# A decoder layer on one core: single-column norm factors move from VectorE to ScalarE, and the FFN weight sums become a step of their own

## The chip, the core and the metric

The kernel runs on one core of a Trainium2 chip. The core's engines work side by side, each on its own instruction queue, and wait for one another by semaphores: PE (TensorE, matmuls and transposes), DVE (VectorE), ACT (ScalarE), POOL (GpSimd) and SP (SyncE, which only issues DMAs here). The metric is the device time of one execution in microseconds. All tensors are float32, one batch of 1024 tokens, width 1024.

## The reference, cut to what matters

The layer has three residual blocks. Before each, every row is normalised: divided by the root of its mean square plus EPS, times a gain.

```python
def rmsnorm(x, g):
    xf = x.astype(jnp.float32)
    y = xf * lax.rsqrt(jnp.mean(xf * xf, axis=-1, keepdims=True) + EPS)
    return (y * g.astype(jnp.float32)).astype(x.dtype)

def reference(x, mem, ...):
    ...
    h = h + token_mixer(rmsnorm(h, g_mix[l]), ...)                       # top-k sparse + differential attention
    h = h + cross_attention(rmsnorm(h, g_xattn[l]), rmsnorm(mem, g_mem[l]), ...)  # 4 heads, 256 memory tokens, w_xo
    h = h + conv_glu(rmsnorm(h, g_ffn[l]), w_ffn_in[l], conv_w[l], conv_b[l], w_ffn_out[l])

def conv_glu(hn, w_ffn_in, conv_w, conv_b, w_ffn_out):
    a, gate = jnp.split(hn @ w_ffn_in, 2, axis=-1)        # 1024 x 1024 times 1024 x 5632
    ...                                                   # causal convolution of width 3 over the tokens
    return (jax.nn.gelu(conv) * gate) @ w_ffn_out
```

## The kernel before

Rows of tokens are handled in eight tiles of 128 (t = 0 to 7). Products in float32 are made of three matmuls each (`mm3`, L287 to L289): every operand is split into a high part, which a cast rounds, and a low part, which is the remainder; high by high, high by low and low by high are added in PSUM. So for each weight and each activation somebody makes a cast (ACT, or POOL) and a subtraction (DVE, or POOL).

**Norm factors.** `rstd` makes 1/sqrt(mean square + EPS) without a square root: a first guess by integer arithmetic on the bits and two polynomial steps. On DVE this is nine instructions (L107, L108, L110 to L116) on a tile of 128 rows by n columns. `norm_rows` calls it with one column, behind an ACT instruction that squares a row tile and sums it (L1113). It is called sixteen times: in `x_norm` for the eight tiles of the cross attention's input, and in `f_norm` for the eight tiles of the FFN's input. In `f_norm` the scaling at L1293 (h times factor times gain, two halves of 512 columns) follows. Other callers of `rstd` have two or more columns.

**The way into the FFN.** `xo_unit(1, t)` is the second half of the cross attention's output projection for tile t: 24 matmuls, and L1278 adds the result to h. In its middle stands `f_tr(t - 2)`, which transposes the scaled tile t − 2 on PE (L1359, two groups of four 128 x 128 transposes, one PSUM bank each of the two banks called trp). For tiles 0 to 3 the banks are split into high and low (cast L1310, subtraction L1313, into B11 and B21). For tiles 4 to 7 one bank is split into B22, and both go into sums and differences for a Strassen-like scheme: L1324 adds high and low back (`xb_sum`), L1372 and L1374 subtract on DVE and read the banks, L1376 and L1378 subtract on POOL. Behind the last tile `xb_finish` splits the sums T1 to T3 (cast L1338, subtraction L1339).

The FFN's input has 22 tiles of 128 columns of a and of the gate (f = 0 to 21). One tile takes seven products of 12 matmuls (`product`), with the weights' sums and differences as one factor and B11, B21, B22, T1 to T4 as the other. Its results pass through three kinds of PSUM buffers (acc, trp, big).

**Weights.** The class `Weights` holds a list of jobs in the order of use. `pump(1)` works off the next job if there is room among the twelve split pages; `get` forces jobs until the pages asked for are there. For one FFN tile there are four jobs: A splits both halves of the first load and, behind that, forms the sums and differences of both loads in place (L204 to L206); B, C and D split the rest (L212 is one more difference). L181 is the cast, L184 the subtraction on DVE. Each load is 512 KB into one of three raw buffers, issued by SP when a buffer comes free.

**What sets the order.** The order of an engine's instructions is fixed when the kernel is built: a scheduler with a model of the chip's times orders DVE, ACT, POOL and SP over the whole program. Only in one block the order of PE is that of the code (`manual_schedule`): there the eight `xo_unit(1, t)` with their transposes, then the first FFN tile, with the last two transposes between its products:

```python
for t in range(NT):
    xo_unit(1, t, (lambda: f_tr(t - 2)) if t >= 2 else None)
    f_norm(t)
first = ffn_in(0)
next(first)
f_tr(6)
next(first)
f_tr(7)
next(first)
```

Each `next` is a product: B11, B21, and B22, which needs tile 7.

Of the kernel before, what the change touches and what calls it, by code (L numbers as in the profile page):

```python
# [12 lines left out]
I32 = mybir.dt.int32  # L13
AF = mybir.ActivationFunctionType
OP = mybir.AluOpType
# [3 lines left out]
P = 128  # L19
T = 1024  # L20
D = 1024
# [5 lines left out]
EPS = 1e-6  # L27
# [17 lines left out]
def hybrid_layer(ctx, tc, I, out):  # L45
    nc = tc.nc
    pe, act, dve, pool, sp = nc.tensor, nc.scalar, nc.vector, nc.gpsimd, nc.sync
# [13 lines left out]
    def nm(s):  # L61
        cnt[0] += 1
        return f"{s}_{cnt[0]}"
# [16 lines left out]
    def small(name, shape=(P, 8), bufs=8):  # L80
        return wpool.tile(list(shape), F32, name=nm(name), tag=name, bufs=bufs)
# [20 lines left out]
    def rstd(eng, r, ss, n, scale):  # L102


        w = small("rst", (P, 3, 8), 4) if n <= 8 else rt("hl", [P, 3, 64], F32, "rstw")
        m, y, t = w[:, 0, :n], w[:, 1, :n], w[:, 2, :n]
        eng.tensor_scalar(m, ss, scale, EPS, op0=OP.mult, op1=OP.add)  # L107
        eng.tensor_scalar(y.bitcast(I32), m.bitcast(I32), -0.5, 1597463007.0, op0=OP.mult, op1=OP.add)  # L108
        if eng is dve:
            eng.scalar_tensor_tensor(t, y, -3.0 / 16, y, op0=OP.mult, op1=OP.mult)  # L110
            eng.tensor_tensor(t, t, m, op=OP.mult)
            eng.scalar_tensor_tensor(y, t, 9.0 / 16, y, op0=OP.add, op1=OP.mult)
            eng.scalar_tensor_tensor(t, y, 64.0 / 9, y, op0=OP.mult, op1=OP.mult)
            eng.tensor_tensor(t, t, m, op=OP.mult)
            eng.scalar_tensor_tensor(t, t, -10.0 / 3, t, op0=OP.add, op1=OP.mult)
            eng.scalar_tensor_tensor(r, t, 5.0, y, op0=OP.add, op1=OP.mult)  # L116
        else:
            eng.tensor_tensor(t, y, y, op=OP.mult)
            eng.tensor_tensor(t, t, m, op=OP.mult)
            eng.tensor_scalar(t, t, -3.0 / 16, 9.0 / 16, op0=OP.mult, op1=OP.add)  # L120
            eng.tensor_tensor(y, t, y, op=OP.mult)
            eng.tensor_tensor(t, y, y, op=OP.mult)
            eng.tensor_tensor(t, t, m, op=OP.mult)
            eng.tensor_scalar(m, t, 64.0 / 9, -10.0 / 3, op0=OP.mult, op1=OP.add)
            eng.tensor_tensor(t, t, m, op=OP.mult)
            eng.tensor_scalar(t, t, 64.0 / 9, 5.0, op0=OP.mult, op1=OP.add)
            eng.tensor_tensor(r, t, y, op=OP.mult)


    NRAW, NWP = 2, 12  # L130

# [12 lines left out]
    class Weights:  # L144
# [41 lines left out]
        def split(self):  # L186
            i = self.nsplit
            key, src, n, engines, kind, _ = self.jobs[i]
            while src is not None and i not in self.raws:
                self.load()  # L190
            raw = self.raws.pop(i, None)
            fi = self.fi

            def fpart(x):
                self.parts(self.page(key), x, 512, engines[0])
            if kind == "A":
                fi["a"] = raw
                fpart(raw[:, 0, :])
                fpart(raw[:, 1, :])
                if i + 1 not in self.raws:  # L200
                    self.load()
                a, g = raw, self.raws[i + 1]
                fi["s"] = s1 = page_s()
                dve.tensor_tensor(s1, g[:, 0, :], g[:, 1, :], op=OP.add)  # L204
                dve.tensor_tensor(g[:, 0, :], a[:, 0, :], g[:, 0, :], op=OP.subtract)
                dve.tensor_tensor(a[:, 0, :], s1, a[:, 0, :], op=OP.subtract)  # L206
            elif kind == "B":
                fi["g"] = raw
                a = fi["a"]
                fpart(a[:, 0, :])  # L210
                fpart(fi["s"])
                dve.tensor_tensor(a[:, 1, :], a[:, 1, :], a[:, 0, :], op=OP.subtract)  # L212
            elif kind == "C":
                fpart(fi["g"][:, 0, :])
                fpart(fi["a"][:, 1, :])
            elif kind == "D":
                fpart(fi["g"][:, 1, :])
            elif kind == "memT":
                for j in range(2):
                    pg = self.page(key)  # L220
                    for b in range(2):
                        v = slice(256 * b, 256 * b + 256)
                        gk = gmem[:, n + 2 * j + b:n + 2 * j + b + 1]
                        act.activation(pg[:, 0, v], raw[:, j, v], AF.Copy, scale=gk)
                        dve.scalar_tensor_tensor(pg[:, 1, v], raw[:, j, v], gk, pg[:, 0, v].bitcast(F32),
                                                 op0=OP.mult, op1=OP.subtract)
            elif kind == "xq":
                for j in range(2):
                    pg, gk = self.page(key), gxa[:, engines + j:engines + j + 1]
                    pool.tensor_scalar(pg[:, 0, :], raw[:, j, :], gk, 1.0, op0=OP.mult, op1=OP.mult)  # L230
                    dve.scalar_tensor_tensor(pg[:, 1, :], raw[:, j, :], gk, pg[:, 0, :].bitcast(F32), op0=OP.mult, op1=OP.subtract)
            else:
                for j in range(2):
                    self.parts(self.page(key), raw[:, j, :n], n, engines[j])
            self.nsplit += 1
            if len(self.raws) < NRAW - 1 + len(raw3) // 2 or self.nload < self.nsplit:
                self.load()
# [17 lines left out]
    W = Weights()  # L255
# [23 lines left out]
    FIW = ("a", "d")  # L279
    for f in range(FT):  # L280
        src = [I["w_ffn_in"][f, :, w, :].rearrange("p (a b) -> p a b", a=2) for w in range(2)]
        W.add(("fi", f), src[0], 512, (FIW,), "A")
        W.add(("fi", f), src[1], 512, (FIW,), "B")
        W.add(("fi", f), None, 512, (FIW,), "C")
        W.add(("fi", f), None, 512, (FIW,), "D", 1)
# [17 lines left out]
    def rt(tag, shape, dt, name):  # L303
        return rot.tile(shape, dt, name=nm(name), tag=tag, bufs=ROT[tag])
# [35 lines left out]
    for k in range(KT):  # L340
        raw = early.tile([P, T], F32, name=nm("xraw"), tag="xr", bufs=5)
# [590 lines left out]
    for s in range(-4, NB):  # L932
        h, i = b_units[max(s, 0)]
        m = s % NT
# [137 lines left out]
    for s in range(-2, NA + 3):  # L1072
        i, h = a_units[min(max(s, 0), NA - 1)]
# [20 lines left out]
        u = s - 2  # L1094
# [16 lines left out]
    def norm_rows(src, jk, ssq, r):  # L1111

        act.activation(jk, src, AF.Square, accum_out=ssq)  # L1113
        rstd(dve, r, ssq, 1, 1.0 / D)

    hx, hx_h = {}, {}

    def x_norm(t, jk):
        ht = kq([P, D], F32, "hld")
        sp.dma_start(ht, h_d[t * P:(t + 1) * P, :])  # L1120
        st = small("st", (P, 12), 6)
        norm_rows(ht, jk, st[:, 0:1], st[:, 1:2])
        dve.tensor_scalar(ht, ht, st[:, 1:2], None, op0=OP.mult)
        hx_h[t] = ht
# [43 lines left out]
    def page_s():  # L1168
        return pgp.tile([P, 512], F32, name=nm("ws"), tag="ws", bufs=1)
# [113 lines left out]
    def f_norm(t):  # L1283
        rs = slice(t * P, (t + 1) * P)
        act.dma_start(h2_d[rs, :], h2[t])
        st = small("st", (P, 12), 6)
        ws = [w2([P, 512], F32, "hn") for _ in range(1 if t >= 4 else 2)]
        norm_rows(h2[t], ws[0].bitcast(BF), st[:, 0:1], st[:, 1:2])
        hn = []
        for g in range(2):  # L1290
            hg = h2[t][:, g * 512:(g + 1) * 512]
            w = hg if t >= 4 else ws[g]
            dve.scalar_tensor_tensor(w, hg, st[:, 1:2], gff[g], op0=OP.mult, op1=OP.mult)  # L1293
            hn.append(w)
        hst[t] = hn
# [420 lines left out]
```

## Time and profile before

| | us |
|---|---|
| median of three runs | 1697.2 (1692.95 to 1699.25) |
| profiled execution | 1697.69 |
| its span, first to last instruction | 1695.9 |
| PE busy in the span | 1570.8 (93%) |
| DVE busy | 1296.0 (76%) |
| ACT busy | 736.7 (43%) |
| POOL busy | 666.8 (39%) |

The granted TensorE clock over the span is 0.977 of full speed. The stages follow each other in time: projections and the first two attentions until about 690 us, cross attention until about 940, the second half of its output projection with f_norm until about 1004, the entry to the FFN, FFN input until about 1475, FFN output until the end. A row of a timeline gives the start, the busy time, the engine, the line in the kernel, the operation, output and input tiles and, in square brackets, how long the engine had been idle and what ended it. A row of waits gives the engine and its waiting line, what it waited for, the sum in us, how often, and the longest.

### The profile page before, as it was taken

Reading aid. Unit: us, or ns where it says so; the run is one execution under the profiler, and the core shown is the slowest. Engines: PE = TensorE matmul, PEld = TensorE weight load, DVE = VectorE, ACT = ScalarE, POOL = GpSimd, SP = SyncE. Lnnn points to the kernel's source line nnn. Section 1 sums busy time; section 2 is a strip of 40 time slices with the busy share of each in tenths; the row PEclk is TensorE's granted clock in tenths of the full one; section 3 lists DMA queues with packets and bytes.
Section 4 is the critical chain, followed back from the end, with each engine's and each line's share of the span. In section 5 each row is a group of like instructions: output and inputs, shape, how many; then the busy total and the mean of one; then the engine's idle time right before and its main releaser. Section 6 shows DMA issues by size and latency. Waiting matters only on the chain.

```text
span 1695.9 us, 22395 instructions
## 1 busy us (share of the span) xinstructions
PE 1570.8 (93%) x7660; PEld 1284.2 (76%) x7660; DVE 1296.0 (76%) x2524; ACT 736.7 (43%) x1469; POOL 666.8 (39%) x908
## 2 busy tenths in 40 slices
PE   8899988878889989999999978999999999899999
PEld 7788766667778778878777766887777777778887
DVE  5736998999999987467553588999988888665554
ACT  6545576566655326325442234333333333343432
POOL 2746666545440230140100032556666566541121
PEclk9999999899989999999999989999999999999999
DMA  8321225222230212261202121555544554698812
GB/s 284 94 82 58 71 93 163 73 62 78 90 100 26 70 68 69 71 220 63 75 25 88 62 87 65 179 174 191 174 164 166 179 180 167 251 366 320 315 50 75
DMA packets 112161, 220.05 MB, mean 130 GB/s; under 512 B 18480, under 2 KB 38448, under 8 KB 112048
## 3 DMA queue, kind: packets, MB, share of 16 engines
q1 hardware_dynamic: 91072, 148.37, 26.5%
q0 software_dynamic: 18384, 61.36, 10.3%
q10 hardware_dynamic: 2592, 8.91, 1.4%
q8 instruction: 60, 0.98, 0.2%
q14 instruction: 53, 0.43, 0.1%
HBM read 160.92 MB, written 57.67 MB: 129 GB/s over the span
## 4 chain that ended last, share of the span: by engine, by line
PE 47%; DVE 31%; DMA 8%; issue 6%; POOL 5%; ACT 3%; SPq 0%; ACTq 0%; DVEq 0%; POOLq 0%
PE acc L287 8%; PE acc L288 8%; PE acc L289 8%; DVE jk L544 6%; DVE wp L184 4%; PE big L288 3%; PE big L287 3%; PE big L289 3%; DMA fs<-u_d 2%; POOL fs L1529 2%; PE trp L287 2%; PE trp L288 2%; PE trp L289 2%; PE big L1255 2%; DMA raw<-in_w_ffn_in_dram 2%
## 5 line engine op out<-in xcount | busy, mean ns | idle before, releaser
L184 DVE TENSOR_TENSOR wp<-raw,wp 128x512 fp32r<-128x512 f32 (+1 forms) x200 | 192.9, 973 | 21.8 <-ACT wp L181 13.2
L181 ACT CAST wp<-raw 128x512 fp32r<-128x512 f32 (+1 forms) x188 | 110.1, 614 | 173.3 <-DVE raw L206 121.4
L1580 DVE TENSOR_TENSOR wp<-fo,wp 128x1024 fp32r<-128x1024 f32 x77 | 100.6, 1322 | 76.8 <-ACT wp L1579 75.2
L1529 POOL TENSOR_TENSOR fs<-fs,fs 128x512 f32<-128x512 f32 x88 | 126.8, 1441 | 77.6 <-DMA fs<-u_d 56.8
L1579 ACT CAST wp<-fo 128x1024 fp32r<-128x1024 f32 x77 | 79.8, 1049 | 108.9 <-PE big L289 47.0
L287 PE MATMUL acc<-wp,xh 128*128 128x512 f32 (+1 forms) x272 | 110.3, 407 | 9.4 <-ACT X L625 9.4
L183 POOL TENSOR_SCALAR wp<-raw 128x512 fp32r<-128x512 f32 (+1 forms) x64 | 46.7, 740 | 177.5 <-DVE rst L110 63.4
L289 PE MATMUL acc<-wp,xl 128*128 128x512 f32 (+1 forms) x272 | 109.8, 404 | 0.0
L288 PE MATMUL acc<-wp,xh 128*128 128x512 f32 (+1 forms) x272 | 109.5, 404 | 0.0
L661 ACT COPY pt<-trp 128x512 f32<-128x512 f32 (+3 forms) x144 | 65.6, 476 | 69.0 <-PE trp L670 68.5
L184 POOL TENSOR_TENSOR wp<-raw,wp 128x512 fp32r<-128x512 f32 x52 | 69.2, 1349 | 45.7 <-ACT wp L181 45.6
L1016 PEld LDWEIGHTS acc<-va_t,pt 128*128 128x128 f32 x576 | 74.0, 195 | 7.1 <-ACT pt L661 5.0
L1016 PE MATMUL acc<-va_t,pt 128*128 128x65 f32 x576 | 76.6, 273 | 2.6 <-ACT pt L661 2.0
L1626 POOL TENSOR_TENSOR hr<-hr,r 128x512 f32<-128x512 f32 x16 | 26.9, 1692 | 123.0 <-DMA fo<-ws_d 59.6
L1061 POOL DMA_DIRECT2D h_d<-xr x16 | 9.3, 579 | 165.6 <-DVE xr L1060 147.3
L999 ACT ACTIVATE ea<-ea,sta 128x128 f32<-128x128 f32 (+7 forms) x64 | 49.3, 777 | 49.8 <-DVE sta L998 46.4
L287 PEld LDWEIGHTS acc<-wp,xh 128*128 128x128 f32 x272 | 53.0, 195 | 23.0 <-ACT X L625 11.6
L544 DVE TENSOR_SCALAR_CACHE_REDUCE jk<-mb,cx 128x640 bf16<-128x640 uint16 (+1 forms) x64 | 68.6, 1072 | 0.7
L1482 POOL TENSOR_TENSOR fg<-fc,fg 128x1024 f32<-128x1024 f32 x21 | 50.9, 2425 | 36.3 <-ACT fc L1477 36.1
L544 DVE TENSOR_SCALAR_CACHE_REDUCE jk<-mb,cand 128x640 bf16<-128x640 bf16 (+3 forms) x60 | 64.4, 1073 | 0.4
L288 PE MATMUL acc<-wp,wp 128*128 128x512 f32 x152 | 61.2, 403 | 2.8 <-DVE wp L184 2.8
L1474 ACT ACTIVATE fc<-fa,cw 128x1024 f32<-128x1024 f32 x22 | 27.4, 1245 | 81.9 <-DVE fa L1433 72.2
(419 smaller groups left out, 5140.6 us busy)
## 6 DMA issues: line engine op xcount, KB each, us to landing
raw<-in_w_ffn_in_dram SPq DMA_DIRECT2D x44, 512.0 KB, 4.2
fs<-in_w_ffn_out_dram POOLq DMA_DIRECT2D x44, 256.0 KB, 3.8
ws_d<-fs POOLq DMA_DIRECT2D x44, 256.0 KB, 2.3
fs<-u_d POOLq DMA_DIRECT2D x44, 256.0 KB, 3.8
us_d<-fs POOLq DMA_DIRECT2D x44, 256.0 KB, 2.9
fo<-us_d SPq DMA_DIRECT2D x44, 256.0 KB, 5.3
fo<-ws_d SPq DMA_DIRECT2D x44, 256.0 KB, 5.4
u_d<-fg POOLq DMA_DIRECT2D x21, 512.0 KB, 4.4
```

Of the source, the lines that this page charges most:

```text
L181: act.copy(pg[:, 0, :n], src)
L184: (dve if el == "d" else pool).tensor_tensor(pg[:, 1, :n], src, pg[:, 0, :n].bitcast(F32), op=OP.subtract)
L287: pe.matmul(o, lhsT=lh, rhs=rh, start=start, stop=False)
L288: pe.matmul(o, lhsT=lh, rhs=rl, start=False, stop=False)
L289: pe.matmul(o, lhsT=ll, rhs=rh, start=False, stop=stop)
L544: dve.tensor_scalar(jk[:, :n], src, th[:, j:j + 1], None, op0=OP.is_ge, op1=OP.add, accum_out=cnt[:, j:j + 1])
L661: act.copy(dst, src)
L1016: pe.matmul(acc[:, hh * 65:hh * 65 + 65], lhsT=pt, rhs=va_t[:, kt, :], start=kt == 0, stop=kt == i)
L1482: pool.tensor_tensor(g, cv, g, op=OP.mult)
L1529: pool.tensor_tensor(o, p, q, op=op)
L1579: act.copy(hi, raw)
L1580: dve.tensor_tensor(lo, raw, hi.bitcast(F32), op=OP.subtract)
```

## The change

`norm_rows` calls a new function `rstd1`. Its first two steps stay on DVE; the rest, seven instructions on DVE before, are ten ACT instructions of one column (`AF.Copy` gives in times scale plus bias). Where a factor is itself a column of the tile, it is passed as the scale, a 128 x 1 operand; that is so in seven of the ten. The job A of the FFN weights ends behind its two splits, and a new job S, without pages of its own, makes the sums; it is a step of its own of `pump`.

```diff
+    def rstd1(r, ss, scale):
+        w = small("rst", (P, 3, 8), 4)
+        m, y, t, u = (w[:, 0, j:j + 1] for j in range(4))
+        dve.tensor_scalar(m, ss, scale, EPS, op0=OP.mult, op1=OP.add)
+        dve.tensor_scalar(y.bitcast(I32), m.bitcast(I32), -0.5, 1597463007.0, op0=OP.mult, op1=OP.add)
+        def mul(o, x, f, bias=0.0):
+            act.activation(o, x, AF.Copy, bias=bias, scale=f)
+        mul(t, y, y)
+        mul(t, t, m)
+        mul(t, t, -3.0 / 16, 9.0 / 16)
+        mul(y, y, t)
+        mul(t, y, y)
+        mul(t, t, m)
+        mul(u, t, 64.0 / 9, -10.0 / 3)
+        mul(t, t, u)
+        mul(t, t, 64.0 / 9, 5.0)
+        mul(r, t, y)
...
                 fpart(raw[:, 0, :])
                 fpart(raw[:, 1, :])
-                if i + 1 not in self.raws:
+            elif kind == "S":
+                while i + 1 not in self.raws:
                     self.load()
-                a, g = raw, self.raws[i + 1]
+                a, g = fi["a"], self.raws[i + 1]
                 fi["s"] = s1 = page_s()
                 dve.tensor_tensor(s1, g[:, 0, :], g[:, 1, :], op=OP.add)
...
         W.add(("fi", f), src[0], 512, (FIW,), "A")
+        W.add(("fi", f), None, 512, (FIW,), "S", 0)
         W.add(("fi", f), src[1], 512, (FIW,), "B")
...
         act.activation(jk, src, AF.Square, accum_out=ssq)
-        rstd(dve, r, ssq, 1, 1.0 / D)
+        rstd1(r, ssq, 1.0 / D)
```

Lines behind the new function are 20 to 22 higher in the kernel after: L184 is L204 there, L204 to L206 are L225 to L227, L1293 is L1315, L1324 is L1346, L1359 is L1381, L1372 and L1374 are L1394 and L1396. The two DVE steps are L133 and L134, the ten ACT steps L137.

The order of DVE ahead of the scaling of tile 6 (`h_1861`; `rst_9902` and `st_9899` are its factor's tiles, `rst_9978` those of tile 7), before:

```order
L112 SCALAR_TENSOR_TENSOR rst_9902<-rst_9902 128x1
L113 SCALAR_TENSOR_TENSOR rst_9902<-rst_9902 128x1
L114 TENSOR_TENSOR rst_9902<-rst_9902 128x1
L107 TENSOR_SCALAR rst_9978<-st_9975 128x1
L115 SCALAR_TENSOR_TENSOR rst_9902<-rst_9902 128x1
L1324 TENSOR_TENSOR xf_10017<-B_1903_9597,B_1905_9599 128x256
...
L116 SCALAR_TENSOR_TENSOR st_9899<-rst_9902 128x1
...
L204 TENSOR_TENSOR ws_10175<-raw_10173 128x512
L184 TENSOR_TENSOR wp_10167<-raw_9565,wp_10167 128x512
L110 SCALAR_TENSOR_TENSOR rst_9978<-rst_9978 128x1
L1293 SCALAR_TENSOR_TENSOR h_1861_9271<-h_1861_9271,st_9899,gff_9351 128x512
```

And after, from the same place to the last reader of tile 6's second bank (`st_9941` is the factor of tile 6, `st_10020` that of tile 7, `h_1862`; `trp_10060` the bank):

```order
L204 TENSOR_TENSOR wp_10215<-raw_9664,wp_10215 128x512
L204 TENSOR_TENSOR wp_10218<-raw_9664,wp_10218 128x512
L226 TENSOR_TENSOR raw_10221<-raw_9664,raw_10221 128x512
L1315 SCALAR_TENSOR_TENSOR h_1861_9295<-h_1861_9295,st_9941,gff_9375 128x512
L1315 SCALAR_TENSOR_TENSOR h_1861_9295<-h_1861_9295,st_9941,gff_9377 128x512
L227 TENSOR_TENSOR raw_9664<-ws_10238,raw_9664 128x512
L1315 SCALAR_TENSOR_TENSOR h_1862_9297<-h_1862_9297,st_10020,gff_9375 128x512
L1315 SCALAR_TENSOR_TENSOR h_1862_9297<-h_1862_9297,st_10020,gff_9377 128x512
...
L233 TENSOR_TENSOR raw_9664<-raw_9664 128x512
...
L1396 TENSOR_TENSOR T_1943_9895<-trp_10060,T_1941_9893 128x2x128
L1396 TENSOR_TENSOR T_1944_9896<-trp_10060,T_1942_9894 128x2x128
```

The norm steps are gone from between, one more L204 (L184 before) and L226 (L205) stand ahead of the scaling of tile 6, and the scaling of tile 7 stands directly behind L227; before, the six last norm steps of tile 7 were spread over the twenty-two rows ahead of it.

The order of ACT in f_norm of tile 3 after (`rst_9735` and `st_9731` are the factor's tiles; the casts belong to the transposes of tile 2):

```order
L1135 ACTIVATE hn_9732,st_9731<-h_1846_9186 128x1024
L137 ACTIVATE rst_9735<-rst_9735 128x1
L1332 CAST B_1900_9618<-trp_9763 128x2x128
L137 ACTIVATE rst_9735<-rst_9735 128x1
L1332 CAST B_1904_9622<-trp_9772 128x2x128
L137 ACTIVATE rst_9735<-rst_9735 128x1
L1332 CAST B_1901_9619<-trp_9763 128x2x128
L137 ACTIVATE rst_9735<-rst_9735 128x1
L1332 CAST B_1905_9623<-trp_9772 128x2x128
L137 ACTIVATE rst_9735<-rst_9735 128x1 x5
L137 ACTIVATE st_9731<-rst_9735 128x1
```

The four casts, which stood alone there before, are now interleaved with the first steps of the chain. On PE one matmul moves: the first of the product with B22 stands directly behind the transposes of tile 7, ahead of the twelve of the second FFN tile's first product, which it followed before.

## Rows read from the trace of the kernel before

**Rows 1.** Windows: us, busy (x instructions) PE, PEld, DVE, ACT, POOL, PEclk, DMA share, GB/s

```profile
980.00:1020.00 40.00, 29.16 (x135) 23.62 (x133) 36.98 (x93) 14.30 (x29) 15.39 (x18) 0.87 0.22 79
1020.00:1060.00 40.00, 35.38 (x143) 27.85 (x144) 35.63 (x53) 18.25 (x29) 9.65 (x9) 0.91 0.21 69
```

**Rows 2.** Waits of PE, 940 to 1060: total us, times, longest

```profile
PE trp L1359 <- issue: 15.1, 2, 8.7
```

**Rows 3.** Timeline of PE, FFN entry: start, us, line, [idle before <-releaser]

```profile
1003.38 0.40 PE L289 MATMUL acc<-B,wp 128*128 128x512 f32 x1
1012.48 1.94 PE L1359 MATMUL trp<-ident,h 128*128 128x128 f32 x8 [8.70 <-issue]
...
1017.69 0.39 PE L289 MATMUL acc<-B,wp 128*128 128x512 f32 x1
1024.49 1.94 PE L1359 MATMUL trp<-ident,h 128*128 128x128 f32 x8 [6.41 <-issue]
...
1033.71 0.39 PE L287 MATMUL trp<-T,wp 128*128 128x512 f32 x1
```

**Rows 4.** Timeline of DVE, FFN entry

```profile
1004.30 0.56 DVE L112 SCALAR_TENSOR_TENSOR rst<-rst 128x1 f32<-128x1 f32 x1
...
1008.10 0.61 DVE L116 SCALAR_TENSOR_TENSOR st<-rst 128x1 f32<-128x1 f32 x1
...
1009.83 1.21 DVE L204 TENSOR_TENSOR ws<-raw 128x512 f32<-128x512 f32 x1
...
1011.63 1.40 DVE L1293 SCALAR_TENSOR_TENSOR h<-h,st,gff 128x512 f32<-128x512 f32 x2
...
1013.56 0.68 DVE L205 TENSOR_TENSOR raw<-raw,raw 128x512 f32<-128x512 f32 x1
...
1016.23 0.74 DVE L1374 TENSOR_TENSOR T<-trp,T 128x256 f32<-128x256 f32 x2
1016.89 1.11 DVE L212 TENSOR_TENSOR raw<-raw 128x512 f32<-128x512 f32 x1
...
1019.13 1.21 DVE L184 TENSOR_TENSOR wp<-ws,wp 128x512 fp32r<-128x512 f32 x1
...
1023.63 1.41 DVE L1293 SCALAR_TENSOR_TENSOR h<-h,st,gff 128x512 f32<-128x512 f32 x2
```

**Rows 5.** Groups of ACT instructions, shapes apart: busy, mean ns | idle before

```profile
L1230 ACT ACTIVATE ex<-big,st 128x256 f32<-128x256 f32 x32 | 17.8, 564 | 20.5 <-DVE st L1227 18.1 <-DVE rst L110 1.5 <-DVE rst L108 0.8
...
L1201 ACT ACTIVATE jk<-q 128x256 bf16<-128x256 f32 x32 | 13.2, 421 | 0.2
...
L334 ACT COPY misc<-misc 128x1 f32<-128x1 f32 x1 | 0.2, 191 | 0.0
```

**Rows 6.** Timeline of DVE, f_norm of tile 0

```profile
960.97 0.15 DVE L108 TENSOR_SCALAR rst<-rst 128x1 int32<-128x1 int32 x1
...
962.52 1.42 DVE L1293 SCALAR_TENSOR_TENSOR hn<-h,st,gff 128x512 f32<-128x512 f32 x2
```

**Rows 7.** Timeline of PE, transposes of tiles 0 and 3

```profile
964.86 1.04 PE L1359 MATMUL trp<-ident,hn 128*128 128x128 f32 x8
...
984.01 1.03 PE L1359 MATMUL trp<-ident,hn 128*128 128x128 f32 x8
```

**Rows 8.** Timeline of ACT, f_norm of tile 3

```profile
978.26 1.67 ACT L1310 CAST B<-trp 128x256 fp32r<-128x256 f32 x4 [0.38 <-PE trp L1359]
```

**Rows 9.** Timeline of DVE, f_norm of tile 3

```profile
977.91 0.15 DVE L107 TENSOR_SCALAR rst<-st 128x1 f32<-128x1 f32 x1 [1.59 <-ACT hn L1113]
...
981.45 0.69 DVE L1278 TENSOR_TENSOR h<-acc,h 128x512 f32<-128x512 f32 x1 [0.27 <-PE acc L289]
982.06 1.41 DVE L1293 SCALAR_TENSOR_TENSOR hn<-h,st,gff 128x512 f32<-128x512 f32 x2
```

**Rows 10.** Waits of PE, 670 to 960 (x_norm)

```profile
PE trp L1133 <- DVE hxl L1136: 2.3, 1, 2.3
```

**Rows 11.** Waits of DVE, 1060 to 1480 (FFN input products)

```profile
DVE ws L204 <- DMA raw<-in_w_ffn_in_dram: 27.6, 16, 3.4
```

## The prediction

> **What bounds the kernel now.** I read the windows by stage first, because shares over the whole span mix stages with different limits. TensorE is busy for the full length of nearly every window; the exception is the entry to the FFN, where two neighbouring windows of 40 us hold only 29.16 and 35.38 us of it, at a granted clock of 0.87 and 0.91 [rows 1]. The reader is to see VectorE there: 36.98 and 35.63 us, the fullest engine. The second view, the waits of TensorE from 940 to 1060, names the place: the transposes at L1359 wait 15.1 us in two waits [rows 2]. "Issue" as the releaser says only that the profile names nothing; the third view, the timelines, shows what stands there. TensorE waits 8.70 us before the transposes of tile 6 at 1012.48 and 6.41 before those of tile 7 at 1024.49 [rows 3], and VectorE starts the scaling of these tiles (L1293, h times the norm factor) at 1011.63 and 1023.63 [rows 4], each time 0.85 us ahead. So the end is set there by VectorE's queue: one stream of norm steps, weight sums (L204 to L212), low halves (L184) and Strassen sums, in a fixed order. Before and behind this place TensorE or the weight loop sets the pace.
>
> **The change, part by part.** Sixteen single-column chains (eight in x_norm, eight in f_norm) lose seven VectorE instructions each and gain ten on ScalarE: 112 out, 160 in. The sums of weights become a step of their own; from the third FFN tile on the order of the engines is that of before, so this part can matter only at the entry.
>
> *Tile 6.* Between 1004.30 and the scaling at 1011.63 lie 7.33 us. Five of the removed steps stand in it, at 0.56 (the first) to 0.61 (the last) each [rows 4], 2.96 us from start to start, and a sixth of 0.07; 4.30 stays. The new order puts one more L184 and the L205 ahead of the scaling, at 0.60 each from start to start: 5.50, so the scaling could start at 1009.8. The steps cost 0.6 there and 0.15 in f_norm of tile 0 [rows 4, 6], and GpSimd is adding beside them. If what they waited for is inherited by their neighbours, five times 0.45 comes back: 1012.0. That is the other end. The Trainium skill, SBUF — State Buffer, section "Who interferes with whom", says that VectorE and GpSimd share a port pair which one holds exclusively; a long and a short step would then wait alike, which the 0.6 against 0.15 bears out. By that rule taking the step away does not take the neighbour's wait away, and the sum would be the later end. I take 1010.9, halfway, 0.7 earlier than before.
>
> *The ScalarE chain.* The trace has no such instruction of one column with a pointer operand. Below it stands the COPY of one column without one, 191 ns; above it an ACTIVATE of 256 columns, 421 ns. The same ACTIVATE with two pointer operands takes 564 [rows 5], so one operand costs about 70 ns: I take 0.27 us for the seven steps with a pointer, 0.19 for the three without, and 0.04 from one dependent step to the next, an estimate. Ten are 2.9 us. The Trainium skill, ScalarE: Activation LUTs, section "What ACT_TABLE_LOAD costs", gives 186 ns plus 0.833 per column and 93 for a pointer operand; by it the ten are 2.5 us busy, and the sum would be the same within 0.2. No run so far shows it. VectorE's seven steps took 1.36 us in f_norm of tile 0 (from 961.16, 0.19 behind 960.97, to 962.52) [rows 6].
>
> *Where the longer chain shows.* Tile 0 of f_norm: scaling from about 964.3, the first half ready at 965.1 and the second at 965.7, against transposes that began at 964.86 [rows 7]: a wait of 0.2 to 0.8, I take 0.6. Tile 3 stands for the steady ones. Its first step starts at 977.91 [rows 9], the two kept steps take until 978.35 with the hop; in the new order the four casts (1.67 us in all) [rows 8] stand between the first four steps of the chain, so 978.35 + 1.67 + 4 times 0.27 + 6 times 0.31 is 982.96. The scaling pair ends 1.33 later, at 984.3; the second half of the transposes is due 0.5 behind 984.01 [rows 7]. So 0.2 is left, and these units cost nothing, where before the scaling began at 982.06, held by L1278 [rows 9]. The cover is thin.
>
> *Tile 7.* Before, the scaling of tile 7 started 12.0 us behind that of tile 6, because its six last norm steps were spread over the queue. Now only L206 stands between (the second fence of the order), 1.9 us. The wait that takes its place is for a PSUM bank: the second half of tile 7's transposes needs tile 6's last L1374 done. Before, that pair began at 1016.23 and L212 at 1016.89 [rows 4], 5.26 behind the scaling of tile 6. Now 1.20 (L184, L205) and 0.13 (two norm steps) leave this stretch; the scaling of tile 7 (1.33), L212 (1.04) and four L184 (two at 0.60, two at 1.13 like the one at 1019.13) come in: 9.8 us. From 1010.9 this is 1020.7, so the second half runs at 1020.8 where it ran at about 1025.45: 4.6 us earlier. The wait of TensorE gets shorter by as much, and some of the slow matmuls behind it go too: eight transposes took 1.94 us here and 1.04 in f_norm [rows 3, 7]; I take 0.8. Against this, the third product's first matmul now stands ahead of the twelve of the second tile's first product and waits for a cast: 0.3. TensorE's next stage, at 1033.71 before [rows 3], starts at about 1028.6: 5.1 us earlier. What is late next are the low halves of the Strassen sums (L1339), which stood 1.7 us ahead of their product and move with the queue.
>
> *x_norm.* TensorE waits there for the low halves that share VectorE and ScalarE with the chain, 2.3 us in one wait [rows 10]. ScalarE's casts come later by up to a chain, VectorE gets lighter. I take 0; doubled it costs 2.3, gone it gives as much.
>
> *Behind the entry.* In the FFN input VectorE waits 27.6 us in 16 waits for weights [rows 11]: the loop of loads, sums and casts paces it, and the loop is started by the same queue. So I let the gain through whole.
>
> *Sum.* −5.1 + 0.6 + 0 = −4.5. The profiled execution took 1697.69 us (span 1695.9 and 1.79 around it), 0.5 above the median of the runs: 1693.2, in round figures 1693. Its own range: entry 3 to 7, tile 0 0 to 0.8, x_norm 2.3 either way: 1688 to 1697.
>
> **Rivals.** *The gain is swallowed.* The loop of the FFN input has its own clock: loads wait for buffers that the casts free, and 27.6 us of waits say that VectorE is early there already. If the first loads don't move, only the 0.6 of tile 0 is left: 1698. For it speak the waits, against it that the last readers of these buffers stand in the same shortened queue.
>
> *Both waits go.* If the transposes of both tiles follow at once, all 15.1 us go, and about 1 of slow clock: 1697.7 − 16 = 1681.6. For it speaks that VectorE is the only cause seen; against it that the work between, 5.5 and 9.8 us, stays on VectorE.
>
> *Slower: ScalarE's chain becomes the bound in every unit of f_norm.* The place is the scaling of tiles 2, 4 and 6 and tile 0: with a step of s instead of 0.27, a chain ends ten times the difference later, the cover being 0.2. A late unit lends its wait to the next, so every second one pays. Tile 0, tile 6 and three others give 50 times (s − 0.27), less 0.6; against the 4.5 gained it decides from s = 0.37. At the upper row, 0.42, it costs 6.9: 1693.2 + 6.9 is 1700. For it speaks the thin cover; against it the 191 ns of one column.
>
> **How the numbers follow.** The forecast 0.50, swallowed 0.22, slower 0.14, both waits gone 0.14. About 0.5% (8.5 us) is what a measurement of this kernel can tell from no change. Below 1688.7 lie the third case and an eighth of the whole from the lower edge of the forecast: 0.27. Above 1705.7 lies only the part of the slower case in which x_norm pays too: 0.09. The rest, 0.64, is no change that can be told. The range reaches to the slower case at one end and halfway to the lost waits at the other: 1685 to 1701.
>
> **What would show it.** Right: transposes of tile 6 at about 1011.7 and of tile 7's second half at about 1021 in the trace after, a step of 0.25 to 0.3 us on ScalarE, TensorE's waits at L1359 down from 15.1 to about 11 (tile 0 among them), an unchanged order and pace from the third tile on. Wrong: waits of TensorE on L1293 in f_norm of a microsecond each, a wait of tile 6 that is longer than 8.7, longer waits for the low halves in x_norm, or a first weight load that lands when it did before.

## The result, and the profile after

The changed kernel takes 1681.22 us (median of six runs, 1678.92 to 1689.94) against 1696.82 of the kernel before (six runs, 1691.88 to 1700.1). The medians lie 15.6 us apart; the ratio, which comes with an interval, is 0.9925 (95%: 0.9903 to 0.9946), or 12.7 us less, and the text goes by it. Two later measurements, each beside the kernel before, gave 0.9926 (0.9910 to 0.9941) and 0.9934 (0.9915 to 0.9952). The forecast was 1693, with a range that ended at 1685. The sign was right, the size was not: nearly three times what was forecast.

The windows at the entry to the FFN, which answer to [rows 1]:

```profile
980.00:1020.00 40.00, 30.59 (x150) 25.28 (x150) 33.07 (x63) 24.83 (x82) 14.76 (x16) 0.92 0.25 92
1020.00:1060.00 40.00, 37.44 (x155) 29.26 (x154) 37.29 (x59) 21.29 (x36) 11.75 (x13) 0.96 0.26 86
```

TensorE gains 3.5 us in the two together and its clock goes up, though the whole stage stands 5 us later than before. VectorE loses only 3.9 us in the first and gains 1.7 in the second. The waits of TensorE from 940 to 1060, after (columns as in [rows 2]):

```profile
PE trp L1381 <- issue: 9.1, 1, 9.1
PE big L310 <- DVE T L1361: 1.2, 1, 1.2
PE trp L1381 <- DVE hn L1315: 1.0, 1, 1.0
PE trp L1381 <- DVE T L1396: 0.9, 1, 0.9
PE acc L309 <- DVE h L1300: 0.6, 1, 0.6
PE big L309 <- ACT B L1332: 0.5, 1, 0.5
```

The two waits of 15.1 us became one of 9.1 ahead of tile 6 and a handful of about a microsecond. Where the profiled executions differ (spans 1678.6 and 1695.9) is best seen by stage. The marks are starts of the same instruction in both timelines; the last column has the same stage in e1, a kernel whose order is that of before:

| from mark to mark | before | after | e1 |
|---|---|---|---|
| start to the first norm square of x_norm | 688.59 | 691.19 | 692.98 |
| to an L1278 of the output projection (939.27) | 250.68 | 251.83 | 252.28 |
| to the L1278 of tile 7 (1002.64 before, 1007.84 after) | 63.37 | 64.82 | 63.37 |
| to the first matmul of trp<-T (1033.71, 1032.57) | 31.07 | 24.73 | 31.03 |
| to the weight sum L204 of the last FFN tile (1434.21, 1422.99) | 400.50 | 390.42 | 390.96 |
| to the first addition of an FFN output (1539.06, 1521.98) | 104.85 | 98.99 | 103.61 |
| to the last such addition | 152.87 | 152.87 | 152.87 |

Three stages are shorter, by 6.3, 10.1 and 5.9 us. But the 10.1 of the FFN input is not the change's: e1, with the order of before, needs 390.96 there too. The profiled execution of the kernel before was a long one in this stage. So one pair of profiles overstates the change by as much as the forecast was in all; what is left to explain is the entry and the end of the FFN input.

### The profile page after: what moved, and what is told of

It is laid out like the page before. It is cut to its first block, busy times and chain, and to the rows that moved or that the text cites. A ratio compares the mean times of both kernels' runs of the same rounds, so it can differ in the third digit from the quotient of the medians.

```text
span 1678.6 us, 22444 instructions
## 1 busy us (share of the span) xinstructions
PE 1567.5 (93%) x7660; PEld 1283.1 (76%) x7660; DVE 1287.5 (77%) x2412; ACT 771.2 (46%) x1629; POOL 669.7 (40%) x908
## 4 chain that ended last, share of the span: by engine, by line
PE 40%; DVE 37%; DMA 9%; issue 5%; ACT 4%; POOL 4%; ACTq 0%; SPq 0%; DVEq 0%; POOLq 0%
PE acc L309 7%; PE acc L310 7%; PE acc L311 7%; DVE jk L566 6%; DVE wp L204 5%; DMA raw<-in_w_ffn_in_dram 3%; PE big L309 2%; PE big L310 2%; PE big L311 2%; DMA fs<-u_d 2%; PE big L1277 2%; DVE fc L1497 2%; DVE fc L1498 2%; DVE e L775 2%; POOL fs L1551 2%
## 5 line engine op out<-in xcount | busy, mean ns | idle before, releaser
L204 DVE TENSOR_TENSOR wp<-raw,wp 128x512 fp32r<-128x512 f32 (+1 forms) x200 | 197.6, 997 | 23.8 <-ACT wp L201 15.2
L1602 DVE TENSOR_TENSOR wp<-fo,wp 128x1024 fp32r<-128x1024 f32 x77 | 105.5, 1386 | 76.0 <-ACT wp L1601 72.8
L204 POOL TENSOR_TENSOR wp<-raw,wp 128x512 fp32r<-128x512 f32 x52 | 69.3, 1350 | 45.6 <-ACT wp L201 45.6
L1499 ACT ACTIVATE fc<-fc 128x1024 f32<-128x1024 f32 x22 | 23.4, 1062 | 86.5 <-DVE fc L1498 86.5
L777 ACT ACTIVATE e<-e,st 128x1024 f32<-128x1024 f32 (+7 forms) x64 | 49.4, 774 | 27.9 <-DVE st L775 27.8
```

The source lines that it names most:

```text
L204: (dve if el == "d" else pool).tensor_tensor(pg[:, 1, :n], src, pg[:, 0, :n].bitcast(F32), op=OP.subtract)
L777: last["act"] = act.activation(e[:, :n], e[:, :n], AF.Exp, bias=st[:, c:c + 1], scale=-1.0, accum_out=st[:, 4 + c:5 + c])
L1602: dve.tensor_tensor(lo, raw, hi.bitcast(F32), op=OP.subtract)
```

## Experiments

**e1: the weight sums alone.** The new job S, with `rstd` on VectorE as before.

> Only the weight sums become a step of their own; the norm factors stay on VectorE. The order of every engine is that of the kernel before. Theory 'order' (what matters is where the rewritten norm steps make the scheduler put things): same as before, 1697 within 5. Rival 'split' (the separate step itself starts loads or casts earlier): 1681 to 1690.

```diff
-        rstd1(r, ssq, 1.0 / D)
+        rstd(dve, r, ssq, 1, 1.0 / D)
```

Ratio 1.0008 (0.9995 to 1.0020). Row by row each engine's order is that of before, so the second part of the change by itself does nothing. The norm factors without it were not run: every kernel below that has `rstd1` has the job S too.

**e2 and e3: the norm factors by stage.** `norm_rows` gets a flag; in e2 only f_norm uses `rstd1`, in e3 only x_norm.

> The new norm factors in f_norm only; x_norm as before. The order of ScalarE and VectorE at the entry to the FFN is like the changed kernel's, while GpSimd's order in the FFN input is that of the kernel before (the first load of each weight sum, fs<-in_w_ffn_out, stands ahead of the multiply fg in every second tile). Theory 'entry' (the gain starts at the entry and the loop only carries it through): 1681 to 1684. Theory 'GpSimd order' (the entry gives about 5 us, the loop's 11 and the 5 at its end come from the load standing behind the multiply): 1690 to 1693, with VectorE's wait for raw at about 27 us and TensorE's wait of 6.9 at the end of the FFN input still there.

> The new norm factors in x_norm only. Both theories: 1 us of loss in x_norm and nothing else, 1698 within 4, since GpSimd's order in the FFN input is that of the kernel before. If x_norm itself gives some of the gain: under 1692.

```diff
-    def norm_rows(src, jk, ssq, r):
+    def norm_rows(src, jk, ssq, r, one=True):
...
-        rstd1(r, ssq, 1.0 / D)
+        if one:
+            rstd1(r, ssq, 1.0 / D)
+        else:
+            rstd(dve, r, ssq, 1, 1.0 / D)
...
```

e2: 0.9970 (0.9957 to 0.9983), 5 us, and far from the changed kernel's 12. Its median of 1687.43 lies between the two theories' figures, but these go by 1697 for the kernel before, which took 1692.12 beside e2: as a difference it is the 4 to 7 us of 'GpSimd order'. Of that theory's signs TensorE's wait at the end stayed, at 4.9 us instead of 6.9. From the L1278 of tile 7 to trp<-T it takes 25.72 us, nearly the changed kernel's 24.73. e3: 0.9989 (0.9974 to 1.0005), no change that can be told, neither the loss that was expected nor a gain. So the entry is worth about 5 us, and the changed kernel has something more that neither part shows alone.

**e4: GpSimd's order in the loop.** The order of GpSimd in the FFN input differs between the kernels: before, from the fourth weight sum of `w_ffn_out` on, the first load of each sum stood ahead of the multiply fg of an FFN tile, after it stands behind. e4 makes that one edge in the kernel before.

> The kernel before with one edge more: the first load of each weight sum (fs<-in_w_ffn_out) is queued behind the multiply fg of the tile before on GpSimd, as in the changed kernel from the fourth sum on. Norm factors and entry as before. Theory 'GpSimd order': 1681 to 1688, VectorE's wait for raw down from 27.6 to 10 to 15. Theory 'entry': 1697 within 4, wait for raw about 27.

```diff
-            pool.tensor_tensor(g, cv, g, op=OP.mult)
+            lastm.append(pool.tensor_tensor(g, cv, g, op=OP.mult))
...
-            owed_sums.extend(fo_sums("w", f // 2))
+            w_sums = fo_sums("w", f // 2)
+            def w_start(start=w_sums[0], m=lastm[f - 1]):
+                with tc.issue_after(m.ins):
+                    start()
+            owed_sums.extend([w_start] + w_sums[1:])
```

1.0009 (0.9997 to 1.0020): nothing. The waits of VectorE from 1060 to 1480 in e4:

```profile
DVE ws L204 <- DMA raw<-in_w_ffn_in_dram: 12.6, 15, 1.9
```

The wait for weights is 12.6 us, as the theory said, and the time did not move. Against the 27.6 of [rows 11] that is less than half, but that execution was a long one: e1, e2, e3 and e8, with the loop's order of before, have 16.1 to 23.8, and three executions of the changed kernel 7.4 to 11.2. The theory fell for the loop: that wait is slack of VectorE, not of the kernel.

**e5: the changed kernel beside e6 to e8.**

> The changed kernel itself, beside the others on one chip. If its gain is the entry (the f_norm part alone gave a ratio of 0.997) and nothing else is there: 0.996 to 0.998. If its order of GpSimd at the end of the FFN input adds a gain of its own: 0.991 to 0.994, with TensorE's wait for fg at the end of the FFN input at about 2 us, where the f_norm part alone has 4.9 and the kernel before 6.9.

0.9926 (0.9910 to 0.9941). So the lead over f_norm alone is real: 0.4%, some 7 us; the two intervals do not meet.

**e6 and e7: the end of the FFN input.** In the stage table the other shorter stage is the end. There, before, VectorE's copy of the last product waits, and TensorE with it. Of the tiles, fa and fg are the two halves of an FFN tile's input product, fc is the convolution, and the multiply fg makes the tile's result, which a store puts into u_d; fs are pieces that GpSimd loads and adds for the output product, fo the pieces that SP loads for it, and wp what ScalarE and VectorE split fo into. The kernel before, ScalarE, GpSimd, VectorE and TensorE around 1480:

```profile
1471.36 1.05 ACT L1579 CAST wp<-fo 128x1024 fp32r<-128x1024 f32 x1 [0.64 <-DMA fo<-in_w_ffn_out_dram]
1482.19 1.24 ACT L1474 ACTIVATE fc<-fa,cw 128x1024 f32<-128x1024 f32 x1 [9.78 <-POOL fg L1482]
```

```profile
1477.04 0.55 POOL L1525 DMA_DIRECT2D fs<-u_d  x1 [0.81 <-DMA us_d<-fs]
1479.24 0.55 POOL L1525 DMA_DIRECT2D fs<-in_w_ffn_out_dram  x1 [1.64 <-DMA us_d<-fs]
1479.80 2.35 POOL L1482 TENSOR_TENSOR fg<-fc,fg 128x1024 f32<-128x1024 f32 x1
```

```profile
1483.46 1.95 DVE L1475 SCALAR_TENSOR_TENSOR fc<-fa,cw,fc 128x1023 f32<-128x1023 f32 x1 [10.83 <-ACT fc L1474]
```

```profile
1486.07 0.80 PE L287 MATMUL acc<-wp 128*128 128x512 f32 x1 [6.86 <-DVE fg L1433]
```

Read backwards: TensorE's first output product waits 6.86 us for VectorE, whose queue stands at L1475 behind ScalarE's fc of tile 21, which waits 9.78 us for GpSimd's multiply fg of tile 20. That multiply stands in GpSimd's queue behind two DMA issues, each of which waits until a store has landed (0.81 and 1.64 us). After, the same chain:

```profile
1462.11 2.40 POOL L1504 TENSOR_TENSOR fg<-fc,fg 128x1024 f32<-128x1024 f32 x1
...
1465.02 0.55 POOL L1547 DMA_DIRECT2D fs<-u_d  x1
1466.18 0.55 POOL L1547 DMA_DIRECT2D fs<-in_w_ffn_out_dram  x1 [0.60 <-DMA us_d<-fs]
```

```profile
1466.29 1.25 ACT L1496 ACTIVATE fc<-fa,cw 128x1024 f32<-128x1024 f32 x1 [6.13 <-DVE fa L1455]
```

```profile
1469.51 0.50 PE L309 MATMUL acc<-wp 128*128 128x512 f32 x1 [1.93 <-DVE fg L1455]
```

The multiply stands ahead of both issues, ScalarE is released by VectorE's fa instead, and TensorE waits 1.93 us. e6 makes that order in the kernel before, e7 in e2.

> The kernel before with one edge more, at the end of the FFN input: the fourth step of the second last sum on GpSimd (its store and the load behind it, which waits for a store to land) is queued behind the multiply fg of FFN tile 20, as in the changed kernel. Theory 'seam' (that multiply stands behind loads that wait, holds ScalarE's fc of tile 21, and so TensorE's first output product): TensorE's wait for fg goes from 6.9 to about 2 to 3 us, and the time to 0.997 to 0.998 of before. Rival (the wait is only handed on to the first fo loads): wait moves elsewhere, same time.

> The new norm factors in f_norm only, x_norm as before, and the last multiply first as in the run before this one. If entry and end are two gains that add: 0.994 to 0.995, 2 us under or level with the changed kernel, since x_norm's loss of about 1 us is gone. If the changed kernel has a third gain in the loop: 2 to 5 us slower than it.

```diff
-            pool.tensor_tensor(g, cv, g, op=OP.mult)
+            lastm.append(pool.tensor_tensor(g, cv, g, op=OP.mult))
...
             def third():
+                if len(lastm) < FT - 1:
+                    one(1, x["11"], x["22"], x["11"])
+                    x["12"] = ld(1, 0)
+                    return
+                with tc.issue_after(lastm[-1].ins):
                     one(1, x["11"], x["22"], x["11"])
                     x["12"] = ld(1, 0)
```

e6: 1.0003 (0.9994 to 1.0011). e7: 0.9978 (0.9965 to 0.9991), no better than e2. The wait was handed on, as the rival had it. ScalarE and TensorE in e6:

```profile
1477.78 1.06 ACT L1477 ACTIVATE fc<-fc 128x1024 f32<-128x1024 f32 x1 [4.34 <-DVE fc L1476]
1488.65 0.33 ACTq L1480 DMA_DIRECT2D u_d<-fg  x1
1489.10 5.78 ACT L1585 CAST wp<-fo 128x1024 fp32r<-128x1024 f32 x6 [10.26 <-DMA fo<-in_w_ffn_out_dram]
```

```profile
1490.19 0.53 PE L287 MATMUL acc<-wp 128*128 128x512 f32 x1 [4.25 <-ACT wp L1585]
```

TensorE no longer waits for fg, but 4.25 us for a cast. ScalarE is idle for 10.26 us; the row names a load as the releaser, but the instruction ahead in its queue is its own store of u_d, issued only at 1488.65, though its data were ready when VectorE's product ended at 1480.1 (1478.87 and 1.22 long). In the changed kernel the same store goes out at 1475.25, 0.03 us behind its data. What held it is in the chain of work that ended last in e6 (start, us, what):

```profile
1482.41 5.89 DMA fo<-in_w_ffn_out_dram
...
1488.32 0.02 ACTq L1480
...
1488.65 0.33 ACTq L1480
```

Ahead of the store ScalarE waits for a second semaphore, the store's own, and in e6 the transfer that had this semaphore last is a load of output weights which SP issued at 1482.41. It landed at 1488.30; then the store went out. In the changed kernel the transfer ahead of the store on its semaphore is another, a load hr<-h_d, which stands earlier in SP's queue there. Before and after:

```profile
1504.34 0.33 SPq L1625 DMA_DIRECT2D hr<-h_d  x1
```

```profile
1469.48 0.32 SPq L1647 DMA_DIRECT2D hr<-h_d  x1
```

It had landed 3.7 us later, 2.1 us before the store's data were ready. All traces with the store on ScalarE agree: in the eight with SP's load at or near its old place (before, e1 to e4, e6 to e8) the store goes out 0.07 to 0.35 us behind the landing of the load of output weights that had its semaphore, in e4 4.6 and in e7 7.0 us behind its data; in the five with the changed kernel's order on SP (after, e5, e14, e9, e15) it goes out 0.03 us behind its data. No run moves SP's load alone.

**e8: tile 7 alone.** `rstd1` for one of the sixteen chains (`t >= 7` as the flag).

> Only the norm factor of tile 7 in f_norm goes to ScalarE, one chain of the sixteen. VectorE's order then has the scaling of tile 7 four instructions behind that of tile 6 and the last readers of tile 6's bank earlier than in the changed kernel. Theory 'tile 7' (the entry's gain is that tile 7's last norm steps no longer stand in VectorE's queue): as much as f_norm alone, 0.996 to 0.998, TensorE's wait ahead of tile 7 down to 2 to 3 us. Rival (all eight chains together unload VectorE): under a fifth of it, 0.999 to 1.0.

0.9957 (0.9943 to 0.9972), as much as all of f_norm. TensorE in e8 at the entry:

```profile
1012.23 1.94 PE L1384 MATMUL trp<-ident,h 128*128 128x128 f32 x8 [8.64 <-issue]
1017.57 1.11 PE L1384 MATMUL trp<-ident,h 128*128 128x128 f32 x8
```

The wait ahead of tile 6 stays at 8.64; that ahead of tile 7, 6.41 before [rows 3], is gone, and these transposes start 5.34 us behind those of tile 6 instead of 12.01. From the L1278 of tile 7 to trp<-T it takes 26.61 us, against 31.07 before and 24.73 in the changed kernel, which loses 1.45 of that again in f_norm. So one short chain taken out of one queue gives the entry's gain, as far as these runs can tell.

**e9: the changed kernel with the multiply moved back** behind the store and the first of the two loads (it stays ahead of the second).

> The changed kernel with one instruction of GpSimd moved back: the multiply fg of FFN tile 20 stands again behind the store and the load of the second last sum, as before; every other engine's order is the changed kernel's. Theory 'end' (this place is worth the changed kernel's lead over the f_norm part alone): TensorE's wait for fg at the end of the FFN input goes from 2 back to 4 to 6 us, ratio 0.9945 to 0.996 instead of 0.9926. Rival (the lead comes from somewhere else): ratio as the changed kernel, 0.992 to 0.9935.

```diff
-        else:
+        elif f == FT - 2:
+            late.append((g, cv, f))
+        else:
             pool.tensor_tensor(g, cv, g, op=OP.mult)
...
+        if late:
+            g_, c_, f_ = late.pop()
+            with tc.issue_after(lastu[-1].ins):
+                pool.tensor_tensor(g_, c_, g_, op=OP.mult)
+            pool.dma_start(u_d[f_ * P:(f_ + 1) * P, :], g_)
...
-            pool.dma_start(t, src(m, odd, half))
+            lastu.append(pool.dma_start(t, src(m, odd, half)))
```

0.9941 (0.9920 to 0.9963), TensorE's wait for fg 3.7 us. The wait grew as expected, the time could not be told from the changed kernel's in e5, another measurement; e15 repeats it.

**e10 and e11: the end without the store in ScalarE's queue.** e6 with the last store issued by GpSimd, where no cast stands behind it; e11 adds e8.

> The kernel before with the last multiply first, as in e6, and the last store of u_d, which held ScalarE from 1478.8 to 1488.7 in e6, issued by GpSimd instead. Theory 'handed on' (e6 gained nothing because ScalarE stood at this store, whose queue slot an earlier transfer held, and the casts for the output products stood behind it): casts start at once, TensorE's 4.2 us wait for wp goes, ratio 0.9965 to 0.998. Rival (the transfers themselves are late, the DMA engines being full): the wait stays, 0.999 to 1.001.

> Tile 7's norm factor alone on ScalarE (0.9957 by itself) together with the last multiply first and the store moved, as in e10. If the two gains are independent: 0.992 to 0.994, level with the changed kernel or up to 2 us faster. If the end gives nothing: 0.9957.

```diff
-            act.dma_start(u_d[f * P:(f + 1) * P, :], g)
+            pool.dma_start(u_d[f * P:(f + 1) * P, :], g)
```

e10: 0.9968 (0.9952 to 0.9983), 5.4 us. ScalarE and TensorE in e10:

```profile
1481.62 1.06 ACT L1477 ACTIVATE fc<-fc 128x1024 f32<-128x1024 f32 x1 [4.34 <-DVE fc L1476]
1482.58 3.88 ACT L1585 CAST wp<-fo 128x1024 fp32r<-128x1024 f32 x4
```

```profile
1479.26 0.50 PE L287 MATMUL acc<-wp 128*128 128x512 f32 x1 [1.17 <-DVE fg L1433]
```

The casts follow at once and no wait for them is left: e6's missing gain was the store at the head of ScalarE's queue. The store itself is late here too, at 1488.33, 4.4 us behind its data, and costs nothing there. (The store moved without the multiply was not run.) e11: 0.9932 (0.9916 to 0.9948): the two gains add, and one chain plus these edges are level with the changed kernel.

**e12 to e15: is that all?** e2 with the end of e10, the same for tiles 6 and 7 only, the changed kernel, and e9 again, on one chip.

> The new norm factors in f_norm only, together with the end as in e10 (last multiply first, last store by GpSimd). If the changed kernel's gain is the entry plus the end and nothing else: the two ratios multiplied, 0.997 by 0.9968, 0.994, and the changed kernel beside it within 0.1%. If the changed kernel has a third gain, in x_norm or in the loop: it stays 0.15% or more ahead.

> As the run before, with the norm factors of tiles 6 and 7 alone on ScalarE: without TensorE's wait for tile 0's longer chain. If the entry needs only the last two tiles: 0.5 to 1.5 us faster than the run before, 0.993 to 0.9935, under the changed kernel at most by 1.

> The changed kernel beside the two before and the one behind it. 0.991 to 0.994 again.

> The changed kernel with the multiply of FFN tile 20 back behind the store and the load, as in e9, now beside the changed kernel. If that place alone is worth something: 0.1 to 0.25% slower than the changed kernel, and TensorE's wait for fg 3.5 to 6 us against 2. If not: equal.

e12: 0.9941 (0.9919 to 0.9963); e14, the changed kernel: 0.9934 (0.9915 to 0.9952). The entry and the end together give its time within what can be measured; a third gain of 1 to 2 us, in the loop or x_norm, is neither shown nor excluded (the loop's stage takes 389.6 to 390.4 us in three executions of the changed kernel, and 387.3 to 400.5 in those with the loop's order of before). e13: 0.9924 (0.9905 to 0.9944), median 1679.62 against 1680.35 of the changed kernel: level, no version beats it by more than the interval. e15: 0.9928 (0.9906 to 0.9949), TensorE's wait for fg 2.3 us as in e14: moving the multiply behind one of the two loads costs nothing here; what is undone in e9 and e15 is only part of the order of before, since the second load, which waited longer there, stays behind the multiply, and SP's load, with which ScalarE's store goes out at once, keeps its new place.

## Why the prediction was right and wrong

*The entry, right as a sum.* The forecast's terms there, −5.1 and +0.6, are −4.5; f_norm alone measured −5 (e2). By the stages the terms are −6.3 (31.07 to 24.73) and +1.45 (63.37 to 64.82), so both were too small and their errors cancel in part. TensorE's waits at the transposes went to 11.3 us (9.1, 1.0, 0.9 and 0.3), forecast about 11.

*Tile 6, wrong.* It was to start 0.7 us earlier. One of the forecast's own signs of being wrong came: TensorE's wait ahead of tile 6 got longer than 8.7 us, 9.11. VectorE after, which answers to [rows 4], and GpSimd beside it:

```profile
1013.06 0.93 DVE L225 TENSOR_TENSOR ws<-raw 128x512 f32<-128x512 f32 x1 [0.20 <-DMA raw<-in_w_ffn_in_dram]
1013.91 0.14 DVE L134 TENSOR_SCALAR rst<-rst 128x1 int32<-128x1 int32 x1
1013.98 2.27 DVE L204 TENSOR_TENSOR wp<-raw,wp 128x512 fp32r<-128x512 f32 x2
1016.17 1.21 DVE L226 TENSOR_TENSOR raw<-raw,raw 128x512 f32<-128x512 f32 x1
1017.30 1.40 DVE L1315 SCALAR_TENSOR_TENSOR h<-h,st,gff 128x512 f32<-128x512 f32 x2
1018.63 0.68 DVE L227 TENSOR_TENSOR raw<-ws,raw 128x512 f32<-128x512 f32 x1
```

```profile
1012.54 4.29 POOL L1346 TENSOR_TENSOR xf<-B,B 128x256 f32<-128x256 f32 x4
```

From the L1278 of tile 7 (1007.84) to the scaling are 9.46 us; before they were 8.99 (1002.64 to 1011.63). The forecast had two ends, 7.2 and 9.4 by the same mark, and took the middle; the later one, in which neighbours inherit what the removed steps waited for, is what came. Two L204 cost 2.27 us here and the L226 1.21, while GpSimd adds until 1016.83; the L227 of the same length, behind that, costs 0.68. The rule of the Trainium skill, SBUF — State Buffer, section "Who interferes with whom", would have given that end; the trace agrees with it (1.21 us for the L226 beside GpSimd's additions, 0.68 for the L227 behind them). No run takes GpSimd's additions away, so the port as the reason is not shown.

*Tile 7, right in its mechanism, its number in part by luck.* TensorE after, which answers to [rows 3]:

```profile
1018.14 1.94 PE L1381 MATMUL trp<-ident,h 128*128 128x128 f32 x8 [9.11 <-issue]
...
1024.33 0.60 PE L1381 MATMUL trp<-ident,h 128*128 128x128 f32 x4
1025.78 0.63 PE L1381 MATMUL trp<-ident,h 128*128 128x128 f32 x4 [0.85 <-DVE T L1396]
...
1032.57 0.39 PE L309 MATMUL trp<-T,wp 128*128 128x512 f32 x1
```

The second half of tile 7 runs 17.94 us behind the mark (forecast 1020.8 − 1002.64 = 18.2), held by the last L1396 of tile 6, the bank that was named. But two misses cancel in it: the scaling of tile 6 came 1.2 us later by that mark than was taken (9.46 against 8.26), and from there to the end of the last L1396 it took 8.3 us instead of 9.8, mostly because the four L204 in that stretch cost 0.60 each and none 1.13. The eight transposes take 0.60 and 0.63 where they took 1.94 [rows 3], so the slow matmuls behind the wait went with it: trp<-T starts 24.73 behind the mark, forecast 26.0.

*The ScalarE chain, right.* The groups of its steps:

```profile
L137 ACT ACTIVATE rst<-rst 128x1 f32<-128x1 f32 x144 | 36.2, 263 | 16.8 <-DVE rst L134 14.2 <-DVE B L1335 0.4
L137 ACT ACTIVATE st<-rst 128x1 f32<-128x1 f32 x16 | 4.7, 292 | 0.6 <-ACT rst L137 0.2
```

The first nine steps have a mean of 263 ns (0.243 us by the forecast, six at 0.27 and three at 0.19), the last, which has a pointer operand, 292 (0.27). By the figures of the Trainium skill, ScalarE: Activation LUTs, section "What ACT_TABLE_LOAD costs", a step with one pointer is estimated at 280 ns; the trace agrees within 12 ns. In f_norm TensorE waits 1.02 us for tile 0 (forecast 0.6; the same wait is 0.3 in e2, 2.5 in e9 and not listed in e5), and then starts the transposes of tiles 1 to 3 in step, 6.38 us apart:

```profile
969.79 1.29 PE L1381 MATMUL trp<-ident,hn 128*128 128x128 f32 x8 [1.02 <-DVE hn L1315]
976.42 1.03 PE L1381 MATMUL trp<-ident,hn 128*128 128x128 f32 x8
982.80 1.03 PE L1381 MATMUL trp<-ident,hn 128*128 128x128 f32 x8
989.18 1.03 PE L1381 MATMUL trp<-ident,hn 128*128 128x128 f32 x8
```

For these tiles the thin cover held, and the rival in which ScalarE's chain becomes the bound is out: its condition, a step of 0.37 us, was not met.

*x_norm at 0, right* within what e3 can tell.

*The step that failed* is "from the third FFN tile on the order of the engines is that of before, so this part can matter only at the entry". It stands there beside the job S, and for that job alone it is true (e1); for the whole change it is not. It held for TensorE and ScalarE. It did not hold for GpSimd, nor for one load on SP, nor quite for VectorE, where two subtractions for the output weights (L1602) each stand ahead of a copy of a product that they followed before (one of the two moves is in e6 and e10 as well); no run shows a price for these. The new chains of x_norm and f_norm together (with either alone, e2 and e3, the end's order is that of before) made the scheduler place GpSimd's multiplies and loads and SP's load differently, up to 450 us behind the last chain. The order of GpSimd at the end of the FFN input, before:

```
L1529 TENSOR_TENSOR fs<-fs,fs     third difference
L1530 DMA us_d<-fs
L1525 DMA fs<-u_d                 waits for a store
L1525 DMA fs<-in_w_ffn_out_dram   waits for a store
L1482 TENSOR_TENSOR fg<-fc,fg     multiply of tile 20
```

and after, in the numbers of before:

```
L1529 TENSOR_TENSOR fs<-fs,fs     third difference
L1482 TENSOR_TENSOR fg<-fc,fg     multiply of tile 20
L1530 DMA us_d<-fs
L1525 DMA fs<-u_d
L1525 DMA fs<-in_w_ffn_out_dram
```

SP's load moved with it, and with that the store on ScalarE was no longer held. The working had 0 for all this. With both obstacles taken away in the kernel before, the multiply moved and the store moved off ScalarE, it is worth 5.4 us (e10); the multiply alone gives nothing (e6). In the changed kernel's own traces the stage from the L204 of the last FFN tile to the first FFN output takes 98.3 to 99.3 us in three executions, against 101.7 to 104.9 in five with the end's order of before (before, e1, e2, e3, e8): about 4 us. The forecast's −4.5 with e10's −5.4 is −9.9; of the measured −12.7 this leaves 2.8, which lies within its interval (−9.2 to −16.5) and has no cause shown.

*The rivals.* "Both waits go" gave 1681.6 and was met almost to the microsecond, by luck: its reason did not happen, the first wait stayed at 9.1 us. "Swallowed" is out: e2 and e8 carry the entry's gain to the end.

## What to carry to other kernels

Where a scheduler sets the order, a local edit is also a new order everywhere behind it: compare each engine's order to the end of the program, and look first for DMA issues that wait and have a computing instruction behind them in the queue. Taking one such instruction forward can hand the wait to the next queue (e6), so test it with the next head of queue moved as well (e10), and see in the trace which earlier transfer a store waits for. And before a stage's difference is put down to a change, look at the same stage in other executions of the same order.

## What the runs showed of the hardware that was not expected

- The same order of instructions took 400.5 us in the FFN input in one execution and 390.96 in another (before and e1), and the start of x_norm, which no variant touches, came between 687.72 and 693.37 us (e8, e2). One place where this arises: at about 603 us TensorE waited 1.72 us in the kernel before and the matmuls behind ran on at 0.39 us; in the changed kernel it waited 2.49, and the next took 0.80 and the following 0.63.
- VectorE's waits for weights were 12.6 us in e4 and 16.1 to 27.6 in five executions with the loop's order of before, with no difference in time that could be told.
- A store of 512 KB in ScalarE's queue held the casts behind it for 8.6 us after its data were ready (e6), because a load that another engine had issued was the last on its semaphore and landed only then.
